# First rows of the input projection: modulation products of tiles 1 to 3 by column groups, x scaled on GpSimd ahead, and x issued before c

## The chip, the cores and the metric

The kernel runs on one core of a Trainium2 chip. The metric is the device time of one execution in microseconds (us); lower is better. TensorE (PE in the profile) does the matrix products, VectorE (DVE), ScalarE (ACT) and GpSimd (POOL) the elementwise work, and SyncE (SP) issues most transfers. "PEld" is the loading of a product's stationary operand, which runs beside the products.

## What is computed

One layer of a flow-matching backbone: adaLN modulation, one large input projection, a bidirectional state-space scan beside a gated MLP, and an output projection. Only the beginning matters here:

```python
sc = silu(c); scc = silu(c_ctx)
shift, scale, gate = split(sc @ w_ada + b_ada, 3)          # and the same from scc for the context
hc = rmsnorm(ctx, g_pre) * (1 + scale_c) + shift_c         # 256 context tokens
hx = rmsnorm(x, g_pre) * (1 + scale) + shift               # 256 latent tokens
zc = hc @ w_in[:, :XBC_W + DT_W];  zx = hx @ w_in          # D = 2048 is the contracted axis
```

Everything is float32. The 512 tokens (context in columns 0 to 255, latent in 256 to 511) are handled together, with the 2048 features cut into 16 tiles of 128 partitions.

## The kernel before

**Layout.** `xT` holds x transposed: 16 feature tiles of 128 x 512 tokens, loaded by four transfers of 1 MB. A product in full float32 precision is made from three faster ones: each operand is split into a rounded part "hi" and a remainder "lo", and hi*hi, hi*lo and lo*hi are added up in PSUM. So h (the normed and modulated x) exists as `hhi[k]` and `hlo[k]`, and a weight tile as `hi_st` and `lo_st`.

**Start.** ACT takes silu of c and c_ctx (`sc2`, 16 KB, into `sc`), which needs one table of functions, and then touches a square root so that the next table is in place. Then x is squared, even tiles on ACT and odd tiles on DVE (seven segments of the later buffer `y` in turn), and PE sums the squares over the features into `pss`, four tiles at a time in four column groups. Between these groups PE runs products that nobody reads (`warm`, tile `psw`). A small chain of transposes, a product `psb`, a root and a reciprocal leaves 1/rms of every token, spread over all partitions, in `rb` (a segment of `y`).

**Rows.** A "row" kt of the first stage is one feature tile: the products of its weights `wst[kt]` (960 columns: 64 for dt, then seven tiles of 128) with h of the same tile, added over all 16 rows in `psdt` (dt) and `psx[0..6]`. Step ("m", i) is one of these weight tiles, i = -1 being dt. Before a row can start, shift and scale of its 128 features must be known. They are products of `sc` with two chunks of `wada` (1 MB each) per tile. For tile 0 and, in pairs, for tiles 4 to 15 `ada_mm` makes them in four column groups of PE straight in PSUM (`psada`), and `ada_fin` reads them with a 32 x 32 block transpose on DVE (`adat`) and two small activations on ACT (`ha` = scale factor, `hb` = shift). For tiles 1 to 3 another way is taken: `ada_rows` multiplies four contracted tiles at once with 256 columns each, `ada_keep` copies the result to SBUF, `ada_sum` adds the four groups with two small products (tile `sel`), and `ada_one` makes `ha` and `hb`. Then `make_h(kt)` does, for the latent half and the context half: DVE xT = xT * ha * rb, ACT hhi = xT + hb, DVE hlo = (xT + hb) - hhi. `split_hi`, `split_dt` and `split_lo` cut the weights into hi and lo.

**Order.** On PE, DVE, ACT and POOL the instructions run in the order in which the program writes them (`manual_schedule`). `row_steps(kt)` gives the order inside row kt, in which the preparation of row n = kt + 1 is woven; NSING = 4 is the number of tiles whose shift and scale are made singly. SP issues its transfers in program order: c, x, then the chunks of `wada` and `wst` in the order of their use, with six buffers for `wada` and three for `wst`.

Of the kernel before, what the change touches and what calls it, by code (L numbers as in the profile page):

```python
# [8 lines left out]
F32 = mybir.dt.float32  # L9
# [3 lines left out]
ALU = mybir.AluOpType  # L13
# [31 lines left out]
def tile_hybrid_ssd_mlp(  # L45
# [126 lines left out]
    def spt(shape, name):  # L172
        return sps.tile(shape, F32, tag="s", name=name)
# [7 lines left out]
    sc2 = stp.tile([P, KT, 2], F32, name="sc2")  # L181
    nc.sync.dma_start(sc2, ccols)

# [25 lines left out]

    def ada_rows(c):  # L210

        u, k0 = c // 2, 8 * (c % 2)
        if k0 == 0:
            ada_ps[u] = spt([P, 512], f"psada{u}")
        ps = ada_ps[u]
        raw = ada_raw.pop(c)
        for kk in range(8):
            g = kk % 4
            nc.tensor.matmul(ps[32 * g : 32 * g + 32, 0:256], lhsT=sc[:, k0 + kk, :], rhs=raw[:, kk * 256 : (kk + 1) * 256],
                             start=k0 == 0 and kk < 4, stop=k0 > 0 and kk >= 4)  # L220

    def ada_keep(u):
        cp = st2.tile([P, 256], F32, tag="cp", name=f"adac{u}")
        nc.vector.tensor_copy(cp, ada_ps[u][:, 0:256])
        ada_ps[u] = cp, ada_ps[u][:, 256:260]

    def ada_sum(u):
        cp, pt = ada_ps[u]
        for q in range(2):
            nc.tensor.matmul(pt[:, 2 * q : 2 * q + 2], lhsT=cp[:, q * P : (q + 1) * P], rhs=sel[:, 0, 0:2],  # L230
                             start=True, stop=True)

    def ada_one(u):
        pt = ada_ps.pop(u)[1]
        nc.scalar.activation(ha[:, u, :], pt[:, 0:2], AF.Identity, bias=bsc1[:, u : u + 1],
                             scale=pc[:, C_GPRE + u : C_GPRE + u + 1])
        nc.scalar.activation(hb[:, u, :], pt[:, 2:4], AF.Identity, bias=pc[:, C_BADA + u : C_BADA + u + 1])

    def ada_mm(ci):
# [12 lines left out]
    def ada_fin(u):  # L252

        ps = ada_ps.pop(u)
        n = 64 * len(UNITS[u])
        ada_ps[u] = tr = st2.tile([P, 128], F32, tag="row", name=f"adat{u}")
        nc.vector.transpose(tr[:, 0:n], ps[:, 0:n])
        ada_ab(u, 0)

    def ada_ab(u, q):  # L260
        kt, tr = UNITS[u][q], ada_ps[u]
        nc.scalar.activation(ha[:, kt, :], tr[:, 64 * q : 64 * q + 2], AF.Identity, bias=bsc1[:, kt : kt + 1],
                             scale=pc[:, C_GPRE + kt : C_GPRE + kt + 1])
        nc.scalar.activation(hb[:, kt, :], tr[:, 64 * q + 32 : 64 * q + 34], AF.Identity,
                             bias=pc[:, C_BADA + kt : C_BADA + kt + 1])
# [7 lines left out]
    def wst_load(kt):  # L273
        w = st3.tile([P, WST], F32, tag="wst", name=f"wst{kt}")
        nc.sync.dma_start(w, wst[kt])
        wraw[kt] = w
# [11 lines left out]
    ada_load2(1)  # L288
    wraw[0] = st3.tile([P, WST], F32, tag="wst", name="wst0")
    for a, b in ((0, WH), (WH, WST)):  # L290
        nc.sync.dma_start(wraw[0][:, a:b], wst[0][:, a:b])
    ada_load(2)
# [10 lines left out]
    def warm(*ns):  # L303
        for n in ns:
            nc.tensor.matmul(psw[:, 0:n], lhsT=ones, rhs=ones[:, 0:1].to_broadcast([P, n]), start=True, stop=True)
# [26 lines left out]
    nc.vector.tensor_copy(ss4.rearrange("p (b i) -> p b i", i=32), bc(rc, 2, 32))  # L332
    nc.vector.transpose(rb, ss4)
    ada_mm(0)
    ada_mm(1)
    warm(512, 512)
    psdt = spt([P, TOK], "psdt")
# [20 lines left out]
    def split_lo(kt, a=64, b=WST):  # L358
        hi, lo = sp0[kt]
        nc.vector.tensor_tensor(lo[:, a - 64 : b - 64], wraw[kt][:, a:b], hi[:, 64 + a : 64 + b].bitcast(F32), op=ALU.subtract)  # L360

    def make_h(kt):
# [18 lines left out]
    def row_steps(kt):  # L381
# [31 lines left out]
    STEPS = {"a": ada_mm, "f": ada_fin, "f2": lambda u: ada_ab(u, 1), "r": ada_rows, "k": ada_keep, "g": ada_sum, "o": ada_one,  # L413
             "h": make_h, "c": split_hi, "d": split_dt, "l": split_lo,
             "l1": lambda n: split_lo(n, 64, WH), "l2": lambda n: split_lo(n, WH)}

# [29 lines left out]
    split_dt(0)  # L446
    make_h(0)
    split_lo(0, 64, WH)
# [813 lines left out]
def _layout(i):  # L1262
# [13 lines left out]
    for kt in range(NSING):  # L1276
        r = ss[:, :, :, kt] if kt == 0 else ss[:, :, :, kt].transpose(0, 1, 3, 2, 4)
        wada[2 * kt : 2 * kt + 2] = r.reshape(2, 8, P, 256).transpose(0, 2, 1, 3).reshape(2, P, D)
    for m in range(NSING, KT, 2):
# [49 lines left out]
```

## Time and profile before

| What | Value |
|---|---|
| median of 3 runs | 989.68 us (989.65 to 989.76) |
| profiled execution, first to last instruction (its span) | 987.9 us |
| the median run beyond that span | 1.8 us |
| PE busy in the span | 978.8 us, 99% |
| ACT, DVE, POOL busy | 495.4, 621.4, 112.5 us |
| transfers, 0 to 20 us and 20 to 60 us | 363 and 419 GB/s, the 16 DMA engines busy 0.91 of the time and all of it |

The profile's own time is its span; no other time is given for that execution, so the 1.8 us are the median run less the span, and stand for what lies before the first and after the last instruction. In the timelines the columns are: start in us, duration in us, engine, line, operation, output tile <- input tiles, shape, count of merged instructions, and in brackets how long the engine had been idle and what ended that.

### The profile page before, as it was taken

The page shows a single profiled execution, that of the slowest core. Times are in us where ns is not written, and L with a number is a line of the kernel's source. Part 1 is how long each engine was busy: PE and PEld are TensorE (multiplying, and loading weights), DVE is VectorE, ACT ScalarE, POOL GpSimd, SP SyncE. Part 2 cuts the span into 40 slices and gives each one's busy share as a digit, 9 for nine tenths or more (in the row PEclk, how much of TensorE's full clock was granted, in tenths as well). Part 3 has the DMA queues.
Part 4 walks back from the last instruction along what each step waited for, and adds up shares of the span by engine and source line. Part 5 has one row for each costly group of instructions (what it writes and reads, how often), then busy time and mean ns, then how long its engine had stood idle before and what let it go on. Part 6 is the DMA issues. An engine that isn't in the chain of part 4 may idle for free.

```text
span 987.9 us, 13929 instructions
## 1 busy us (share of the span) xinstructions
PE 978.8 (99%) x5502; PEld 792.6 (80%) x5502; DVE 621.4 (63%) x949; ACT 495.4 (50%) x762; POOL 112.5 (11%) x162
## 2 busy tenths in 40 slices
PE   9999999999999999999999999999999999999997
PEld 4688888778887878787888888887888888888885
DVE  4444488868886566756767766767555564445636
ACT  4233358566665554545445343454565563346522
POOL 0000002432453222224000000000000000000000
PEclk9999999999999999999999999999999999999999
DMA  9999844233323424145877768774455446556722
GB/s 372 421 418 418 352 149 166 86 129 128 128 75 139 142 98 145 43 169 206 297 302 284 275 257 296 280 274 170 170 180 203 171 170 213 178 206 228 282 86 85
DMA packets 31985, 207.26 MB, mean 210 GB/s; under 512 B 4128, under 2 KB 4384, under 8 KB 8496
## 3 DMA queue, kind: packets, MB, share of 16 engines
q1 hardware_dynamic: 29232, 192.79, 52.0%
q0 software_dynamic: 2112, 12.65, 3.7%
q8 instruction: 43, 0.70, 0.3%
q10 hardware_dynamic: 576, 0.94, 0.3%
q14 instruction: 22, 0.18, 0.1%
HBM read 204.20 MB, written 2.16 MB: 209 GB/s over the span
## 4 chain that ended last, share of the span: by engine, by line
PE 92%; DMA 4%; ACT 2%; DVE 1%; SPq 0%; issue 0%; ACTq 0%
PE pa L1108 12%; PE pa L1110 12%; PE pa L1109 12%; PE psx L141 9%; PE psx L143 9%; PE psx L142 9%; PE pm L1157 3%; PE pm L1155 3%; PE pm L1156 3%; DMA wst<-in_wst_dram 3%; PE pq L1157 2%; PE pq L1156 2%; PE pq L1155 2%; PE psada L249 2%; PE psc L778 1%; PE pso L831 1%
## 5 line engine op out<-in xcount | busy, mean ns | idle before, releaser
L85 DVE TENSOR_TENSOR lo_w<-w,hi_w 128x1024 fp32r<-128x1024 f32 x173 | 210.7, 1224 | 146.0 <-ACT hi_w L84 145.9
L84 ACT CAST hi_w<-w 128x1024 fp32r<-128x1024 f32 x173 | 182.1, 1053 | 204.5 <-PE pa L1110 129.4
L1108 PE MATMUL pa<-hi_w,hhi 128*128 128x512 f32 x512 | 202.3, 395 | 0.0
L1110 PE MATMUL pa<-hi_w,hlo 128*128 128x512 f32 x512 | 199.5, 390 | 0.0
L1109 PE MATMUL pa<-lo_w,hhi 128*128 128x512 f32 x512 | 199.3, 389 | 0.0
L141 PE MATMUL psx<-hhi,hi_w 128*128 128x512 f32 (+1 forms) x400 | 153.4, 383 | 0.0
L143 PE MATMUL psx<-hhi,lo_w 128*128 128x512 f32 (+1 forms) x400 | 145.9, 365 | 0.0
L142 PE MATMUL psx<-hlo,hi_w 128*128 128x512 f32 (+1 forms) x400 | 145.7, 364 | 0.0
L1108 PEld LDWEIGHTS pa<-hi_w,hhi 128*128 128x128 f32 x512 | 96.2, 188 | 20.5 <-issue 1.6
L1110 PEld LDWEIGHTS pa<-hi_w,hlo 128*128 128x128 f32 x512 | 96.1, 188 | 20.3
L1109 PEld LDWEIGHTS pa<-lo_w,hhi 128*128 128x128 f32 x512 | 96.2, 188 | 19.5 <-issue 0.2
L576 DVE SCALAR_TENSOR_TENSOR xbc<-psx,pc,xbc 128x248 f32<-128x248 f32 (+1 forms) x204 | 83.6, 473 | 34.8 <-ACT xbc L560 33.9
L501 DVE TENSOR_TENSOR lo_w<-w,hi_w 128x1024 fp32r<-128x1024 f32 x61 | 77.1, 1271 | 23.7 <-ACT hi_w L495 23.6
L141 PEld LDWEIGHTS psx<-hhi,hi_w 128*128 128x128 f32 x400 | 75.5, 189 | 13.4 <-issue 2.9
L143 PEld LDWEIGHTS psx<-hhi,lo_w 128*128 128x128 f32 x400 | 75.4, 188 | 12.5
L142 PEld LDWEIGHTS psx<-hlo,hi_w 128*128 128x128 f32 x400 | 75.6, 189 | 12.2 <-issue 1.7
L495 ACT CAST hi_w<-w 128x1024 fp32r<-128x1024 f32 x61 | 63.5, 1044 | 26.0 <-PE psx L142 12.9
L966 DVE SCALAR_TENSOR_TENSOR junk<-gate,cb 128x2048 bf16<-128x2048 f32 x16 | 36.7, 2291 | 24.1 <-DMA gate<-in_wada_dram 24.1
L1155 PE MATMUL pm<-hi_w,hhi 128*128 128x512 f32 x128 | 50.0, 390 | 0.0
L1156 PE MATMUL pm<-lo_w,hhi 128*128 128x512 f32 x128 | 49.9, 390 | 0.0
L1157 PE MATMUL pm<-hi_w,hlo 128*128 128x512 f32 x128 | 49.7, 389 | 0.0
L730 ACT ACTIVATE R<-R,y 128x128 f32<-128x128 f32 x128 | 38.8, 391 | 0.0
(248 smaller groups left out, 1333.6 us busy)
## 6 DMA issues: line engine op xcount, KB each, us to landing
w<-in_wlat_dram SPq DMA_DIRECT2D x64, 1024.0 KB, 4.8
w<-in_wout_dram SPq DMA_DIRECT2D x32, 1024.0 KB, 4.8
ada<-in_wada_dram SPq DMA_DIRECT2D x30, 1024.0 KB, 13.4
w<-in_wxbc_dram SPq DMA_DIRECT2D x25, 1024.0 KB, 4.8
gate<-in_wada_dram SPq DMA_DIRECT2D x16, 1024.0 KB, 5.5
R<-acs POOLq DMA_DIRECT2D x8, 1024.0 KB, 5.2
wst<-in_wst_dram SPq DMA_DIRECT2D x15, 480.0 KB, 14.0
xT<-in_xch_dram SPq DMA_DIRECT2D x4, 1024.0 KB, 8.0
```

Of the source, the lines that this page charges most:

```text
L84: nc.scalar.copy(hi, raw)
L85: nc.vector.tensor_tensor(lo, raw, hi.bitcast(F32), op=ALU.subtract)
L141: nc.tensor.matmul(ps, lhsT=whi, rhs=hhi[k][:, s], start=start, stop=False)
L142: nc.tensor.matmul(ps, lhsT=whi, rhs=hlo[k][:, s], start=False, stop=False)
L143: nc.tensor.matmul(ps, lhsT=wlo, rhs=hhi[k][:, s], start=False, stop=stop)
L576: nc.vector.scalar_tensor_tensor(ao, zi, cw[:, k : k + 1], ao, op0=ALU.mult, op1=ALU.add)
L1108: nc.tensor.matmul(pa[tk], lhsT=hhi[k][:, t], rhs=whi[:, w], start=k == 0, stop=False)
L1109: nc.tensor.matmul(pa[tk], lhsT=hhi[k][:, t], rhs=wlo[:, w], start=False, stop=False)
L1110: nc.tensor.matmul(pa[tk], lhsT=hlo[k][:, t], rhs=whi[:, w], start=False, stop=k == KT - 1)
L1155: nc.tensor.matmul(p, lhsT=yh[:, t], rhs=whi[:, w], start=j == 0, stop=False)
L1156: nc.tensor.matmul(p, lhsT=yh[:, t], rhs=wlo[:, w], start=False, stop=False)
L1157: nc.tensor.matmul(p, lhsT=yl[:, t], rhs=whi[:, w], start=False, stop=hf == 0 and j == 15)
```

## The change

Five things are changed, all of them ahead of row 4.

1. Tiles 1 to 3 take the way of tile 0: `ada_mm` with 64 columns and four column groups, `ada_fin` with the transpose from PSUM. `ada_rows`, `ada_keep`, `ada_sum` and `ada_one` go. For tiles 0 to 3 `ha` is now made on DVE, while ACT makes `hb`.
2. xT * rb of tiles 0 to 3 is done on GpSimd (`scale_x`), queued right behind the making of `rb`.
3. For tiles 0 to 3 `make_hs` replaces `make_h`: ACT hhi = xT * ha + hb in one activation; DVE makes the same value in float32 (`full`, a segment of `y`) and subtracts.
4. The order in rows 0 to 3 is another: row 0 has products by token halves and a list of its own (`row0`), and in rows 1 and 2 both chunks of the next tile, `ada_fin`, h and the splits stand behind weight tile 4 (`m[:6]`); the weight transfers of tiles 1 to 3 are issued in two parts.
5. c (`sc2`) is issued from ACT, behind `pc`; x is now SP's first transfer. The last `warm` before row 0 has 256 columns in place of 512.

```diff
-    nc.sync.dma_start(sc2, ccols)
+    nc.scalar.dma_start(sc2, ccols)
...
-    def ada_rows(c):
...
-    def ada_keep(u):
...
-    def ada_sum(u):
...
-    def ada_one(u):
...
     def ada_fin(u):
...
         nc.vector.transpose(tr[:, 0:n], ps[:, 0:n])
-        ada_ab(u, 0)
+        if u < NSING:
+            nc.vector.tensor_scalar(ha[:, u, :], tr[:, 0:2], pc[:, C_GPRE + u : C_GPRE + u + 1], bsc1[:, u : u + 1],
+                                    op0=ALU.mult, op1=ALU.add)
+            nc.scalar.activation(hb[:, u, :], tr[:, 32:34], AF.Identity, bias=pc[:, C_BADA + u : C_BADA + u + 1])
+        else:
+            ada_ab(u, 0)
...
     def wst_load(kt):
         w = st3.tile([P, WST], F32, tag="wst", name=f"wst{kt}")
-        nc.sync.dma_start(w, wst[kt])
+        for a, b in ((0, WH), (WH, WST)) if kt < NSING else ((0, WST),):
+            nc.sync.dma_start(w[:, a:b], wst[kt][:, a:b])
...
+    def scale_x(kt):
+        for s in TH:
+            nc.gpsimd.tensor_tensor(xT[:, kt, s], xT[:, kt, s], rb[:, s], op=ALU.mult)
+
+    TH = (slice(256, 512), slice(0, 256))
+    for kt in range(2):
+        scale_x(kt)
     ada_mm(0)
     ada_mm(1)
-    warm(512, 512)
+    warm(512, 256)
...
+    def make_hs(kt):
+        full = yseg(2 + kt % 2)
+        for v, s in enumerate(TH):
+            nc.scalar.activation(hhi[kt][:, s], xT[:, kt, s], AF.Identity, bias=hb[:, kt, v : v + 1],
+                                 scale=ha[:, kt, v : v + 1])
+        for v, s in enumerate(TH):
+            nc.vector.tensor_scalar(full[:, s], xT[:, kt, s], ha[:, kt, v : v + 1], hb[:, kt, v : v + 1],
+                                    op0=ALU.mult, op1=ALU.add)
+            nc.vector.tensor_tensor(hlo[kt][:, s], full[:, s], hhi[kt][:, s].bitcast(F32), op=ALU.subtract)
...
+        if n == 1:
+            return [("o", 0), m[5], ("a", 2), m[4], ("a", 3), ("c1", 1), ("f", 1), ("d", 1), ("hs", 1), ("l1", 1),
+                    ("c2", 1), ("l2", 1), m[6], m[7]]
         if n < NSING:
-            r = [("r", 2 * n), ("r", 2 * n + 1)]
-            g = m[4:5] + [("g", n), ("o", n), h_]
-            if n < 3:
-                q = 5 - n
-                return m[:q] + r + [c_, ("k", n), d_, ("l1", n)] + g + [("l2", n)] + m[q:4] + m[5:]
-            return m[:3] + r + s_ + [("k", n)] + g + m[3:4] + m[5:]
+            return m[:6] + [("a", 2 * n), ("a", 2 * n + 1), ("x", n), ("c1", n), ("f", n), ("d", n), ("hs", n),
+                            ("l1", n), ("c2", n), ("l2", n)] + m[6:]
...
+    def row0(kt):
+        whi, wlo = sp0[kt]
+        for v, s in enumerate(TH):
+            nc.tensor.matmul(psdt[:, s], lhsT=whi[:, 0:P], rhs=hhi[kt][:, s], start=v == 0, stop=False)
+            for i in range(3):
+                nc.tensor.matmul(psx[i][:, s], lhsT=whi[:, (i + 1) * P : (i + 2) * P], rhs=hhi[kt][:, s],
+                                 start=v == 0, stop=False)
+        dt_mm(kt, 1)
+        for i in range(3):
+            nc.tensor.matmul(psx[i], lhsT=whi[:, (i + 1) * P : (i + 2) * P], rhs=hlo[kt], start=False, stop=False)
+        for i in range(3):
+            nc.tensor.matmul(psx[i], lhsT=wlo[:, i * P : (i + 1) * P], rhs=hhi[kt], start=False, stop=False)
```

How the order on the engines changes, at three places. First the head of ACT's program, up to the squares of x, in the changed kernel (its line numbers are its own; `sc2` is printed as sc_161):

```order
L104 DMA pc_87<-in_pcols_dram 128x304
L182 DMA sc2_161<-in_ccols_dram 128x32
L272 ACT_TABLE_LOAD
L272 ACTIVATE sc_159<-sc2_161 128x16x2
L273 ACT_TABLE_LOAD
L273 ACTIVATE sc2_161<-epsc_157 128x1
L290 ACTIVATE y_68<-xT_156 128x512 x8
```

The second row is new on this engine; before, it was SP's first transfer, ahead of the four of xT.

Then DVE in the changed kernel, from the transpose that makes rb (first row) to the last split of row 0's weights (wst0, hi_st0 and lo_st0 are the weights of row 0; y is here `full`, or rb in the first row):

```order
L308 STREAM_TRANSPOSE y_68<-y_68 128x512
L228 STREAM_TRANSPOSE adat0_328<-psada0_251 128x64
L230 TENSOR_SCALAR ha_111<-adat0_328,pc_87,bsc1_112 128x2
L338 TENSOR_TENSOR hi_st0_325<-wst0_177,hi_st0_325 128x64
L350 TENSOR_SCALAR y_68<-xT_156,ha_111,hb_110 128x256
L352 TENSOR_TENSOR hlo0_133<-y_68,hhi0_117 128x256
L350 TENSOR_SCALAR y_68<-xT_156,ha_111,hb_110 128x256
L352 TENSOR_TENSOR hlo0_133<-y_68,hhi0_117 128x256
L342 TENSOR_TENSOR lo_st0_326<-wst0_177,hi_st0_325 128x384
L342 TENSOR_TENSOR lo_st0_326<-wst0_177,hi_st0_325 128x512
```

Before, two products of three operands and two subtractions stood in the place of the four rows of L350 and L352, and `ha` was ACT's. POOL's eight products of `scale_x` follow one another beside these rows.

Last PE in the changed kernel, from the end of row 1 to the start of row 2 (psada2 belongs to tile 2, hhi1 to row 1, hhi2 to row 2):

```order
L143 MATMUL psx4_323<-hhi1_118,lo_st1_436 128x512
L220 MATMUL psada2_482<-ada_4_188,sc_159 32x64 x32
L220 MATMUL psada2_482<-ada_5_190,sc_159 32x64 x32
L141 MATMUL psx5_324<-hhi1_118,hi_st1_435 128x512
L142 MATMUL psx5_324<-hlo1_134,hi_st1_435 128x512
L143 MATMUL psx5_324<-hhi1_118,lo_st1_436 128x512
L141 MATMUL psx3_322<-hhi1_118,hi_st1_435 128x256
L142 MATMUL psx3_322<-hlo1_134,hi_st1_435 128x256
L143 MATMUL psx3_322<-hhi1_118,lo_st1_436 128x256
L422 MATMUL psdt_318<-hhi2_119,hi_st2_549 128x512
L439 MATMUL psx0_319<-hhi2_119,hi_st2_549 128x512
L440 MATMUL psx0_319<-hhi2_119,lo_st2_550 128x512
```

Before, the products of tile 2 stood behind weight tile 1 and a pair of 128 x 2 products (`ada_sum`) followed three products behind them, with half of row 1 still to come; now six products of row 1 lie between the last product of tile 2 and the first that needs its h.

More of the change, by code (lines that the diff above doesn't have):

```diff
@@ L208, in tile_hybrid_ssd_mlp @@
     ada_ps = {}
-    def ada_rows(c):
[L212 to L220, printed above, removed]
-    def ada_keep(u):
-        cp = st2.tile([P, 256], F32, tag="cp", name=f"adac{u}")
-        nc.vector.tensor_copy(cp, ada_ps[u][:, 0:256])
-        ada_ps[u] = cp, ada_ps[u][:, 256:260]
-    def ada_sum(u):
[L228 to L231, printed above, removed]
-    def ada_one(u):
[L234 to L237, printed above, removed]
     def ada_mm(ci):
@@ L288, in tile_hybrid_ssd_mlp @@
     ada_load2(1)
-    wraw[0] = st3.tile([P, WST], F32, tag="wst", name="wst0")
-    for a, b in ((0, WH), (WH, WST)):
-        nc.sync.dma_start(wraw[0][:, a:b], wst[0][:, a:b])
+    wst_load(0)
     ada_load(2)
@@ L446, in tile_hybrid_ssd_mlp @@
     split_dt(0)
-    make_h(0)
+    make_hs(0)
     split_lo(0, 64, WH)
@@ L1276, in _layout @@
     for kt in range(NSING):
-        r = ss[:, :, :, kt] if kt == 0 else ss[:, :, :, kt].transpose(0, 1, 3, 2, 4)
-        wada[2 * kt : 2 * kt + 2] = r.reshape(2, 8, P, 256).transpose(0, 2, 1, 3).reshape(2, P, D)
+        wada[2 * kt : 2 * kt + 2] = ss[:, :, :, kt].reshape(2, 8, P, 256).transpose(0, 2, 1, 3).reshape(2, P, D)
     for m in range(NSING, KT, 2):
```

4 lines of the change are left out of this document (2 added, 2 removed).

## The prediction

> **What bounds the kernel now.** I read the chain of waits on the page first, then the engines' busy time in the stretch behind the changed rows, then the timeline from 0 to 60 us. The page and the stretch (its columns: time on PE, PEld, DVE, ACT, POOL, each with its count, then granted clock, DMA share, GB/s):
>
> ```profile
> span 987.9 us, 13929 instructions
> PE 92%; DMA 4%; ACT 2%; DVE 1%; SPq 0%; issue 0%; ACTq 0%
> 60.00:130.00 70.00, 69.95 (x894) 60.00 (x893) 33.96 (x70) 28.31 (x56) 0.00 (x0) 1.00 0.91 375
> ```
>
> PE has 92% of the chain, and behind the changed rows it works 69.95 of 70.00 us at full clock. Nothing there can give time back: what PE loses or wins by row 3 reaches the end whole. The sum is made against the profiled execution (span 987.9); the median, 989.68, lies 1.8 us above it, and I add the same 1.8.
>
> A win has a ceiling, though. Row 5's weights come off a stream of transfers that has no pause yet:
>
> ```profile
> 57.38 0.99 ACT L352 CAST hi_st<-wst 128x960 fp32r<-128x960 f32 x1 [0.60 <-DMA wst<-in_wst_dram]
> 59.69 0.19 PEld L436 LDWEIGHTS psx<-hhi,lo_st 128*128 128x128 f32 x1 [0.33 <-DVE lo_st L360]
> ```
>
> ACT waited 0.60 us for those weights, and PE's loads 0.33 us for what DVE made of them. Rows that start earlier only meet this wait earlier. The stream itself moves up by no more than the place that c leaves at SP's head (x now starts at 1.25, c at 0.81, in rows below): 0.44 us. So no version of these rows can win more than about 0.4.
>
> **The change part by part. First, c behind pc.** The beginning:
>
> ```profile
> 0.81 0.38 SPq L182 DMA_DIRECT2D sc<-in_ccols_dram  x1
> 0.81 0.41 ACTq L104 DMA_DIRECT2D pc<-in_pcols_dram  x1
> 1.25 2.09 SPq L279 DMA_DIRECT2D xT<-in_xch_dram  x4
> 3.02 1.28 ACT L297 ACT_TABLE_LOAD   x1 [3.02 <-DMA sc<-in_ccols_dram]
> 5.86 0.20 ACT L298 ACTIVATE sc<-epsc 128x1 f32<-128x1 f32 x1
> 6.17 1.15 ACT L315 ACTIVATE y<-xT 128x512 f32<-128x512 f32 x2
> 6.95 1.61 PE L317 MATMUL pss<-y,ones 128*32 128x512 f32 x8
> 8.75 1.15 ACT L315 ACTIVATE y<-xT 128x512 f32<-128x512 f32 x2 [1.44 <-DMA xT<-in_xch_dram]
> 15.13 1.07 PE L317 MATMUL pss<-y,ones 128*32 128x512 f32 x8
> 18.67 0.71 DVE L333 STREAM_TRANSPOSE y<-y 128x512 f32<-128x512 f32 x1
> ```
>
> ACT loads its first table only when c has landed (3.02), and the two tables, silu and the touch of the root end at 5.86 + 0.20 = 6.06. So from c's landing to the first square of x lie 3.04 us, and x lands just then (first square 6.17): in this kernel the two are balanced. In the changed one c is ACT's second transfer, issued at about 0.81 + 0.41 + 0.05 = 1.27, when SP has issued the first MB of x (0.81) and is issuing the second: four issues in 2.09 us are 0.52 each with their gaps, so about 1.3. When does c land?
>
> It is 16 KB, with three bounds. Low: with nothing before it, as now, 2.2 us after issue, at 3.45. Middle: behind one MB of x, which lands 0.44 earlier than now, at about 5.7. High: behind two, 8.75 - 0.44 = 8.3. Two places in the middle of the kernel show what a small or young transfer does when another queue is full. The first has `gate` on SP's queue while q0 (loads of POOL) is at work, the second `G` on POOL's queue while q1 is:
>
> ```profile
> 463.90 0.33 SPq L78 DMA_DIRECT2D gate<-in_wada_dram  x1
> q0 software_dynamic: 242, 0.80, 93.7%
> gate<-in_wada_dram SPq DMA_DIRECT2D x1, 1024.0 KB, 6.7
> 643.88 0.54 POOL L974 DMA_DIRECT2D G<-in_gpost_dram  x1 [80.51 <-ACT hi_w L84]
> q1 hardware_dynamic: 106, 0.87, 78.8%
> G<-in_gpost_dram POOLq DMA_DIRECT2D x1, 1024.0 KB, 7.4
> ```
>
> In the three microseconds from 463.9 only q0 moved a packet, in those from 643.9 only q1; the younger transfer landed 6.7 and 7.4 us after its issue. So the older work is finished first, and c doesn't slip between x's packets: I rule the low bound unlikely. Between middle and high the two issues are about 0.03 us apart, a tie by the rows. c is spread over the 16 engines and has landed when the last share has; one engine that takes x's second tile first is enough for 8.3. I take the high bound.
>
> [...] The trace at 463.9 speaks against strict turns: q1 had work and got none for 3 us.
>
> By the high bound ACT is free at 8.3 + 3.04 = 11.35 in place of 6.06, the first square shifts from 6.17 to 11.35, and PE's first sum of squares from 6.95 to about 12.1. Nothing is caught up: PE's three groups from 6.95 to 15.13 take 2.7 us each with the unread products between them, ACT's two squares of a group 1.15, and x is long there. The last group and with it `rb` (19.38 = 18.67 + 0.71) shift by **5.2 us**. By the middle bound ACT is free at 8.8, the shift is 2.6; by the low one 6.5, and 0.3.
>
> **Second, row 0.** Now from `rb` (call it R, 19.38) to the product of row 1 that waits for nothing more, 31.38, are 12.0 us. The rows of the operations that replace or join those of today:
>
> ```profile
> 19.75 0.25 DVE L257 STREAM_TRANSPOSE adat<-psada 128x64 f32<-128x64 f32 x1 [0.37 <-PE psada L249]
> 20.33 0.28 ACT L264 ACTIVATE hb<-adat,pc 128x2 f32<-128x2 f32 x1
> 20.46 0.88 DVE L365 SCALAR_TENSOR_TENSOR xT<-xT,ha,y 128x256 f32<-128x256 f32 x2
> 21.04 0.91 ACT L368 ACTIVATE hhi<-xT,hb 128x256 fp32r<-128x256 f32 x2 [0.43 <-DVE xT L365]
> 21.58 0.89 DVE L370 SCALAR_TENSOR_TENSOR hlo<-xT,hb,hhi 128x256 fp32r<-128x256 f32 x2 [0.24 <-ACT hhi L368]
> 31.38 0.39 PE L436 MATMUL psx<-hhi,lo_st 128*128 128x512 f32 x1
> 31.61 0.40 PE L418 MATMUL psdt<-hlo,hi_st 128*128 128x512 f32 x1
> L614 DVE TENSOR_SCALAR y<-y 128x256 f32<-128x256 f32 x1 | 0.3, 286 | 0.0
> L823 POOL TENSOR_TENSOR y<-xk,dsk 128x256 f32<-128x256 f32 x16 | 9.5, 610 | 0.0
> 181.72 2.48 POOL L707 TENSOR_TENSOR xw<-xk,ed 128x256 f32<-128x256 f32 x4
> 182.14 2.21 DVE L814 SCALAR_TENSOR_TENSOR M<-cbf,dtt,M 128x128 f32<-128x128 f32 x4
> L814 DVE SCALAR_TENSOR_TENSOR M<-cbf,dtt,M x64: 339/346/698, 182.1 to 452.4; 128x128 f32<-128x128 f32 x64
> ```
>
> DVE's two products (0.88) leave; POOL makes them at 0.61 each, so the two tiles that follow R take 4 x 0.61 = 2.4 us; those of tiles 2 and 3 come in their rows and have time. DVE's new `full` is priced by L614, 0.29 each: 0.57 more than nothing, where the products saved 0.88. By these rows alone row 0 would shorten: ACT needs only POOL's half and `hb`, and I get R + 10.35, a win of 1.65 (hhi starts 0.6 earlier than behind two products of DVE, and lo_st 1.05 earlier than behind two hlo of 0.89).
>
> [...] The four L814 that lie beside POOL's products at 182.14 take 2.21 us, 0.55 each, where their median is 346 ns; one took 698. [...] Turn by turn, with one POOL product between two of DVE: transpose and ha end at R + 0.85, the split of dt 0.6 later; hhi ends at R + 1.4 and R + 2.0; two full (0.29) and two hlo (0.48, each with a wait of 0.61) end DVE's h at R + 4.15; lo_st of 0.55 and 0.68 with what is left of POOL's at R + 5.05 and R + 6.1; PE's products of the three weight tiles that need lo_st at R + 9.1, and the product of row 1 that stands at 31.38 now at R + 11.85, 12.0 now: **-0.15**. The bounds are -1.65 (no lock) and +1.7 (all of POOL's go first); I take the turns, since the four at 182.14 show neither a standstill nor free running.
>
> **Third, rows 1 to 3.**
>
> ```profile
> 28.80 0.55 DVE L360 TENSOR_TENSOR lo_st<-wst,hi_st 128x384 fp32r<-128x384 f32 x1
> 38.31 0.40 PE L418 MATMUL psdt<-hhi,hi_st 128*128 128x512 f32 x1
> 42.72 0.61 PE L230 MATMUL psada<-sel,adac 128*128 128x2 f32 x4
> 45.71 0.40 PE L418 MATMUL psdt<-hhi,hi_st 128*128 128x512 f32 x1
> ```
>
> A row takes 45.71 - 38.31 = 7.40 us now without a wait. The small sums (0.61 on PE) go, with a copy on DVE; that the products of the next tile are now 64 columns wide I take as no difference (at worst it eats the 0.6). But they moved to the end of the row. What follows their last product is a chain: transpose (0.25), hb (0.28), two hhi (0.91), a full and two hlo (0.29 + 0.48), lo_st (0.55), 2.76 us together. PE has six products of row 1 to run meanwhile, three of 512 columns at the pitch of 31.61 - 31.38 = 0.23 and three of 256 at half of it (1.05), then two of row 2 (0.46) and about 0.25 for handing over, before it needs lo_st: 1.75. PE stands for 1.0 and has saved 0.6: **+0.45 for a row**, twice **+0.9** (the third such row, row 1, is in the second part). Today the 3.0 us from L230 (42.72) to the next row (45.71) hide the shorter chain behind it; that cover is gone. The bounds: -0.6 (lo_st, whose weights lie there, made before h after all) and +1.0 (nothing saved). The smaller `warm` and the split transfers of wst are free: both lie beside the chain to `rb`.
>
> Sum: 987.9 + 5.2 - 0.15 + 0.9 + 1.8 = **995.6 us**.
>
> **Rivals.** *c behind one tile of x only:* 2.6 in place of 5.2: 993.1. For it speaks that the two issues nearly tie; against it that all 16 shares must win the tie. *The clock falls:* with the high bound PE stands idle from 7.0 to 12.1. Before its first warm-up its products are slower:
>
> ```profile
> 4.70 0.34 PEld L305 LDWEIGHTS psw<-ones 128*128 128x128 f32 x1 [0.52 <-issue]
> 5.55 0.21 PEld L305 LDWEIGHTS psw<-ones 128*128 128x128 f32 x1 [0.52 <-issue]
> 6.00 0.19 PEld L305 LDWEIGHTS psw<-ones 128*128 128x128 f32 x1 [0.24 <-issue]
> ```
>
> The pitch is 0.85 us up to 5.55 and 0.45 from there. The slow stretch is at most 5.55 - 0.81 = 4.7 us long; run again, it loses 1 - 0.45/0.85 = 0.47 of that, 2.2 us: 997.9. Nothing in the rows shows so long a pause of PE, so I can't say whether it cools. [...]
>
> *The other side, no loss:* c lands early (3.45), from its place on a queue of its own with little in it; then the first part gives +0.3, the second, without the lock, -1.65, the third +0.9, and the ceiling leaves -0.4 of their sum: 989.3; with the turns of row 0 kept it is +1.05, 990.7. It decides where c lands before about 3.5. Against it stand 463.9 and 643.9. *The change does not do what it says:* POOL's products so hinder DVE that x ahead costs as much as it saves; that is the +1.7 above, 997.4 with the high bound.
>
> **How the numbers follow.** High bound 0.40, one tile 0.25, with a cold clock 0.15, c early 0.17, anything else (POOL first) 0.03. The time is that of the likeliest, 995.6. The range reaches from the middle of the early case, 990.0, to the cold one with some slack, 998.2. About 0.2% (2.0 us) is what a measurement of this kernel can tell from no change: the slower cases are 0.40 + 0.25 + 0.15 less 0.08 for a smaller shift, with the other 0.03: 0.75. Early c is mostly within 2.0: with those 0.08 it makes 0.21 for the same, and 0.04 is left for faster, since the ceiling allows it only if the stream should move up more than I see.
>
> **What would show it.** In the changed profile the row of ACT's first table load names c and its time: 8.3 (one tile: 5.7; early: 3.4). PE's first sum of squares stands at 12.1, the transpose that makes `rb` ends at 24.6. The granted clock between 12 and 17 tells the cold case. POOL's eight products behind `rb` and the length of DVE's beside them (over 0.5 us, where alone 0.3) show the lock. From the first psdt of row 2 to that of row 3 should be 7.85 us with PE waiting for `lo_st` or `hhi` for about 1.0. Wrong would be: a first square before 8.5, no wait of PE at the heads of rows 2 and 3, or a wait at row 5 longer than now.

## The result, and the profile after

The changed kernel takes 1001.67 us (median of 4 runs, 1000.76 to 1002.44) where the kernel before takes 989.72: a ratio of 1.0116, with a 95% interval of 1.0104 to 1.0129. It is slower, as forecast in sign, but by about twice the amount (11.5 us by the ratio, 11.95 by the medians, 5.9 forecast) and outside the range. The ratios here and below leave out one execution at a reduced clock, of the kernel before with 64-column products (1222.79 us at a granted clock of 0.75, one of six). The profiled execution of the changed kernel took 1000.76, with this span and chain of waits on the page:

```profile
span 999.0 us, 14523 instructions
PE 93%; DVE 2%; ACT 2%; DMA 1%; issue 1%; ACTq 0%; SPq 0%; DVEq 0%
```

PE still carries the chain, but DVE and "issue" have a larger part in it (1% and 0% before) and DMA a smaller one (4% before): "issue" is time in which the engine waited for nothing that the profile shows. The timeline of the changed kernel, at the places where the loss arises (line numbers are its own):

```profile
1.25 0.45 ACTq L182 DMA_DIRECT2D sc<-in_ccols_dram  x1
9.02 1.28 ACT L272 ACT_TABLE_LOAD   x1 [9.02 <-DMA sc<-in_ccols_dram]
12.63 2.44 PE L292 MATMUL pss<-y,ones 128*32 128x512 f32 x8 [5.18 <-ACT y L290]
25.82 0.71 DVE L308 STREAM_TRANSPOSE y<-y 128x512 f32<-128x512 f32 x1
26.68 6.83 POOL L311 TENSOR_TENSOR xT<-xT,y 128x256 f32<-128x256 f32 x8 [23.67 <-DVE y L308]
27.56 0.72 DVE L350 TENSOR_SCALAR y<-xT,ha,hb 128x256 f32<-128x256 f32 x1
30.01 0.76 DVE L352 TENSOR_TENSOR hlo<-y,hhi 128x256 fp32r<-128x256 f32 x1
30.69 2.23 DVE L342 TENSOR_TENSOR lo_st<-wst,hi_st 128x384 fp32r<-128x384 f32 x2
30.82 0.50 PE L422 MATMUL psdt<-hlo,hi_st 128*128 128x512 f32 x1 [1.26 <-DVE hlo L352]
39.28 0.50 PE L440 MATMUL psx<-hhi,lo_st 128*128 128x512 f32 x1 [0.56 <-DVE lo_st L342]
45.26 0.41 PE L220 MATMUL psada<-ada,sc 128*32 128x64 f32 x11 [0.80 <-issue]
47.54 0.50 PE L422 MATMUL psdt<-hhi,hi_st 128*128 128x512 f32 x1 [0.63 <-ACT hhi L347]
48.95 0.50 PE L440 MATMUL psx<-hhi,lo_st 128*128 128x512 f32 x1 [0.67 <-DVE lo_st L342]
57.45 0.50 PE L440 MATMUL psx<-hhi,lo_st 128*128 128x512 f32 x1 [0.56 <-DVE lo_st L342]
```

The first product of each row that needs `lo_st` (L440, before the change L436) makes a good milestone. Before, it stands at 31.38, 38.78, 46.18 and 55.01 for rows 1 to 4; now at 39.28, 48.95, 57.45 and 66.37. The rows of these that neither stand above nor in the prediction (L436 before, L440 after):

```profile
38.78 0.39 PE L436 MATMUL psx<-hhi,lo_st 128*128 128x512 f32 x1
46.18 0.39 PE L436 MATMUL psx<-hhi,lo_st 128*128 128x512 f32 x1
55.01 0.40 PE L436 MATMUL psx<-hhi,lo_st 128*128 128x512 f32 x1
66.37 0.40 PE L440 MATMUL psx<-hhi,lo_st 128*128 128x512 f32 x1
```

| Stretch | before | after | lost |
|---|---|---|---|
| start to `rb` | 19.38 | 26.53 | 7.15 |
| `rb` to row 1's milestone | 12.00 | 12.75 | 0.75 |
| row 1 to row 2 | 7.40 | 9.67 | 2.27 |
| row 2 to row 3 | 7.40 | 8.50 | 1.10 |
| row 3 to row 4 | 8.83 | 8.92 | 0.09 |

These sum to 11.36; the span grew by 11.1, since the wait for weights at row 5 (0.33) is gone. Nothing is lost or won later.

The first stretch falls into two. PE's first sum of squares moved from 6.95 to 12.63, by 5.68, because c landed at 8.94 and ACT's first table load began at 9.02. From there to `rb` it was 12.43 and is now 13.90, 1.47 more. The granted clock is in the third column from the right. The first row is the kernel before, the other two the changed kernel:

```profile
12.00:18.00 6.00, 6.00 (x67) 2.42 (x69) 2.77 (x6) 1.88 (x4) 0.00 (x0) 1.00 0.99 394
6.00:12.00 6.00, 1.45 (x3) 0.21 (x1) 2.79 (x7) 2.94 (x5) 0.00 (x0) 0.82 1.01 424
12.00:18.00 6.00, 5.37 (x20) 1.56 (x20) 1.29 (x2) 3.28 (x7) 0.00 (x0) 0.61 1.00 397
```

In the changed kernel PE worked 1.45 of the 6 us from 6 to 12, and the granted clock was 0.61 in the next six, where it was 1.00 before.

### The profile page after: what moved, and what is told of

Read it like the earlier page. It is cut to its first block, busy times and chain, and to the rows that moved or that the text cites. A ratio compares the mean times of both kernels' runs of the same rounds, so it can differ in the third digit from the quotient of the medians.

```text
span 999.0 us, 14523 instructions
## 1 busy us (share of the span) xinstructions
PE 980.0 (98%) x5782; PEld 794.6 (80%) x5782; DVE 623.8 (62%) x954; ACT 494.5 (50%) x761; POOL 119.3 (12%) x170
## 4 chain that ended last, share of the span: by engine, by line
PE 93%; DVE 2%; ACT 2%; DMA 1%; issue 1%; ACTq 0%; SPq 0%; DVEq 0%
PE pa L1112 12%; PE pa L1113 12%; PE pa L1114 12%; PE psx L141 9%; PE psx L143 9%; PE psx L142 9%; PE pm L1159 3%; PE pm L1161 3%; PE pm L1160 3%; PE psada L220 3%; PE pq L1161 2%; PE pq L1159 2%; PE pq L1160 2%; PE psc L782 1%; PE pso L835 1%; PE psy L861 1%
## 5 line engine op out<-in xcount | busy, mean ns | idle before, releaser
L580 DVE SCALAR_TENSOR_TENSOR xbc<-psx,pc,xbc 128x248 f32<-128x248 f32 (+1 forms) x204 | 83.6, 472 | 34.8 <-ACT xbc L564 33.9
```

What stands on the lines that cost most here:

```text
L580: nc.vector.scalar_tensor_tensor(ao, zi, cw[:, k : k + 1], ao, op0=ALU.mult, op1=ALU.add)
```

## The experiments

Three theories were tested first: late c (with a cold clock behind it), the rows' own waits, and the transfers' queue. Each ratio is to executions of the kernel before that were made along with that experiment, whose medians lie between 989.78 and 990.49; compare experiments by their ratios.

**c first again, all else as changed.**

```diff
-    nc.scalar.dma_start(sc2, ccols)
+    nc.sync.dma_start(sc2, ccols)
```

> The changed kernel with one edit undone: c is SP's first transfer again, ahead of x. Theory L (late c): c lands near 3.0 in place of 8.94, rb ends near 19.4 in place of 26.5, and 7.2 us of the 12.0 go; the rest of the loss, about 4.1 us by the row starts, stays: about 994. Rival R (rows): the late start is mostly slack that rows 1 to 3 would have lost to their own waits anyway (h and lo_st at the head of each row, transfers that wait for buffers), and the time stays above 998. Rival Q (queue): the waits of rows 1 and 2 are themselves an effect of the late start, because SP stood 5.9 us for row 0's lo_st; then they go too and the time falls to 991 or less.

Measured: 994.89, ratio 1.0043 (1.0026 to 1.0059). The edit of c thus costs some 7 us of the 11.5 (1.0116 less 1.0043), as the table says. The rest stays, so rivals R and Q both fall. In this profile c is back, but PE pauses longer inside the products of tile 2, and then its clock falls, to a mean of 0.55 from 42 to 48 us:

```profile
3.04 1.28 ACT L272 ACT_TABLE_LOAD   x1 [3.04 <-DMA sc<-in_ccols_dram]
38.77 0.41 PE L220 MATMUL psada<-ada,sc 128*32 128x64 f32 x11 [1.52 <-issue]
42.00:48.00 6.00, 5.80 (x16) 4.32 (x15) 1.02 (x2) 0.00 (x0) 0.00 (x0) 0.55 1.01 412
```

The profiled execution was the longest of the four (996.53; the shortest 993.94), and such a fall of the clock fits a scatter of that size. The mean clock of the four executions goes with it: 0.996, 0.997, 0.998 and 0.999 for 996.53, 995.64, 994.14 and 993.94 us. That it is the cause was not tested.

**Only c behind pc, on the kernel before.**

```diff
-    nc.sync.dma_start(sc2, ccols)
+    nc.scalar.dma_start(sc2, ccols)
```

> The kernel before with one edit of the change alone: c is issued by ACT behind pc. Theory L: c lands near 8.9, first square of x near 12, rb shifts by 7.2 as in the changed kernel, and the time is 989.7 + 7.2 = 996.9. Rival (c lands in time when nothing else is changed, or the rows take up the shift): below 992.

Measured: 995.91, ratio 1.0057 (1.0042 to 1.0072): one moved line of 16 KB costs 5.6 us by itself (6.9 in the profiled execution, the longest of the four, by its span of 994.8). c lands as late as in the changed kernel, PE's clock halves, and rows 1 to 3 keep their 7.50 and 7.40 us:

```profile
9.30 1.28 ACT L297 ACT_TABLE_LOAD   x1 [9.30 <-DMA sc<-in_ccols_dram]
12.00:18.00 6.00, 5.08 (x12) 1.56 (x12) 1.29 (x2) 3.56 (x8) 0.00 (x0) 0.50 1.01 420
```

With the 4.3 of the experiment before (the change without this line) it makes 9.9 of 11.5. Each of the three has an interval of more than 1 us to either side, so the remaining 1.6 us are not clear of the noise.

**c ahead of pc on ACT.** Changed kernel, the two issues of ACT exchanged:

```diff
+    nc.scalar.dma_start(sc2, ccols)
     nc.scalar.dma_start(pc, pcols)
...
-    nc.scalar.dma_start(sc2, ccols)
```

> The changed kernel with ACT's two transfers exchanged: c first, pc second; x stays SP's first. Theory of turns (an engine finishes a tile of x, then takes one transfer of the other queue, then the next tile): c lands where pc lands now, at 6.4, and pc at about 8.9; ACT is free at 9.5, rb shifts by 4 to 4.5 rather than 7.15, PE idles about 2.7 us and stays warm: about 998. Theory of arrival: c comes at the same moment as x's first tile and shares with it, lands before 4, and the time is that of c first or lower, 993 to 994.

Measured: 998.61, ratio 1.0081 (1.0066 to 1.0096). c landed with the first tile of x, not before it, as the theory of turns has it (how long a turn is, the last experiment tells). That PE would stay warm was wrong: it idled only 2.07 us, and the clock was halved right behind, from 10.5 to 13.9 us:

```profile
6.22 1.28 ACT L272 ACT_TABLE_LOAD   x1 [6.22 <-DMA sc<-in_ccols_dram]
10.50:13.90 3.40, 3.40 (x8) 1.00 (x5) 2.47 (x6) 2.10 (x4) 0.00 (x0) 0.50 1.01 426
```

**PE kept at work until c is there.**

```diff
     warm(512, 512, 512, 512)
+    warm(*[512] * 6)
```

> The changed kernel with six more unread products (512 columns, about 0.87 us each warm) behind the first four, so that PE works through its pause from 6.86 to 12.63. Theory C (cold clock): the granted clock from 12 to 18 is 1.00 in place of 0.61, the first group of sums and its unread products take 2.6 to 3.0 us in place of 4.67, and the time falls by 1.3 to 2.2, to about 999.5 to 1000.4, with less scatter between runs. Rival: the clock is not what makes that stretch long, and the time stays within 0.5 of 1001.7 or grows.

Measured: 1000.88, ratio 1.0107 (1.0092 to 1.0123), just above the range expected, and not clear of the changed kernel's 1.0116 (1.0104 to 1.0129). The clock theory holds for its stretch: the clock stays at 1.00, and `rb` ends at 25.30 in place of 26.53. But something took most of the 1.2 us back: PE's pause that waits for nothing grew from 0.80 to 3.02 us and moved, from the products for tile 2's shift and scale to a product of row 0's weight tile 5.

```profile
12.00:18.00 6.00, 4.93 (x22) 1.61 (x23) 2.14 (x4) 4.42 (x10) 0.00 (x0) 1.00 1.00 419
38.31 0.39 PE L142 MATMUL psx<-hlo,hi_st 128*128 128x512 f32 x1 [3.02 <-issue]
```

That a pause moves when products are added far ahead of it suggests that it hangs on a count. So the next theory, K, was that PE stops for its own code.

**Rows 1 and 2 prepared early.** c first, and:

```diff
-            return m[:6] + [("a", 2 * n), ("a", 2 * n + 1), ("x", n), ...] + m[6:]
+            return m[:2] + [("a", 2 * n), ("a", 2 * n + 1), ("x", n), ...] + m[2:]
```

> c first on SP as in the first experiment, and in rows 1 and 2 the whole preparation of the next tile stands behind two steps of the row (dt and weight tile 0) in place of six. Theory H (heads of rows): PE's waits at the heads of rows 2 and 3 (1.5 us each for hhi and lo_st) go, so 2 x 1.5 us less, and the clock, which fell to 0.55 from 42 to 48 us there, stays at 1.00 (up to 2.3 more): 990.5 to 992. Rival K (code): PE's pause inside the products of tile 2 is where the time goes; the heads matter little, the pause stays at the same count of instructions or longer, and the time is above 993.

Measured: 994.42, ratio 1.0043 (1.0029 to 1.0057): nothing won. The waits at the heads of rows 2 and 3 are gone, as theory H wants, but the pause of PE grew to 3.31 us, as rival K wants.

**GpSimd held back in row 0.** c first, and GpSimd's products of tile 1 (and all behind them) wait for row 0's splits:

```diff
-    for kt in range(2):
-        scale_x(kt)
+    scale_x(0)
...
     split_lo(0, WH)
+    nc.gpsimd.tensor_copy(scr, sp0[0][1][:, WST - 65 : WST - 64].bitcast(F32))
+    scale_x(1)
```

> c first on SP, and GpSimd's four products of tile 1 wait (behind a one-element copy of the last column of row 0's lo_st) until DVE has finished row 0's splits. Theory P (DVE and GpSimd exclude each other): DVE's full, hlo and lo_st of row 0 fall from 0.72-0.82, 0.77 and 1.15 us to about 0.41, 0.43 and 0.6, PE's wait for the second hlo (1.4) shrinks by 0.8 or more, and row 1 starts 0.8 to 1.3 earlier: 993.5 against 994.9. Rival: only GpSimd is slowed, DVE keeps its lengths, no change within 0.5.

Measured: 992.17, ratio 1.0024 (1.0015 to 1.0033); without the edit it was 1.0043 (1.0026 to 1.0059), so the gain in time is at the edge of the noise. Row 1 starts 1.25 us earlier (29.52 for 30.77), within what was expected. The timeline of row 0:

```profile
20.29 0.72 DVE L349 TENSOR_SCALAR y<-xT,ha,hb 128x256 f32<-128x256 f32 x1
21.12 0.42 DVE L351 TENSOR_TENSOR hlo<-y,hhi 128x256 fp32r<-128x256 f32 x1
21.46 0.41 DVE L349 TENSOR_SCALAR y<-xT,ha,hb 128x256 f32<-128x256 f32 x1
22.32 1.15 DVE L341 TENSOR_TENSOR lo_st<-wst,hi_st 128x384 fp32r<-128x384 f32 x2
23.67 4.19 POOL L311 TENSOR_TENSOR xT<-xT,y 128x256 f32<-128x256 f32 x6
```

With GpSimd at rest, DVE's `full`, `hlo` and the two `lo_st` take 0.41, 0.42 and 1.15 us (the first `full`, 0.72, still lies beside the two products of tile 0, which end at 20.86); beside it they took 0.72 to 0.82, 0.76 and 2.23. GpSimd's products are hindered too: six take 4.19 here, 0.70 each, where the eight of the changed kernel took 6.83, 0.85 each. Theory P holds as far as these lengths go: each engine's operations are longer beside the other's. That the two exclude each other was not shown. The heads of rows keep their waits. This profile has no pause for code, which would account for more than P alone was to win.

**The kernel before with 64-column products for tiles 1 to 3**, at their old places (`ada_mm` and `ada_fin` in place of `ada_rows`, `ada_keep`, `ada_sum` and `ada_one`, with the order of `wada` in memory that goes with them):

```diff
-            r = [("r", 2 * n), ("r", 2 * n + 1)]
-            g = m[4:5] + [("g", n), ("o", n), h_]
+            r = [("a", 2 * n), ("a", 2 * n + 1)]
+            g = m[4:5] + [("f", n), h_]
```

> The kernel before with one part of the change alone: tiles 1 to 3 by column groups (64 products of 64 columns and the transpose from PSUM), at the places in rows 0 to 2 where their products stood before. Theory K (code): PE runs 128 instructions more per tile, its code is fetched in pieces of 16 KB behind 1 MB transfers, and a pause of PE of 0.8 to 2 us that waits for nothing in the records appears in rows 1 or 2, ending 1.3 us behind a piece; net of the 0.6 us per row of the small sums the time is 989.5 to 991.5. Rival: no pause, and 3 x 0.6 us are saved up to the ceiling of the transfers: 989.2 to 989.5.

Measured: 993.02, ratio 1.0031 (1.0019 to 1.0044), slower than K had priced it: there are two pauses "issue" (0.87 us at 38.51 and 1.42 at 46.15), and at the head of row 1 PE waits 1.85 us for `hhi`. That wait comes from DVE's order: the transpose of tile 1 stands behind a split of the weights, whose rounding on ACT waited for their transfer until 27.64, while tile 1's products were done at about 27.4.

```profile
29.28 0.24 DVE L257 STREAM_TRANSPOSE adat<-psada 128x64 f32<-128x64 f32 x1
31.52 0.50 PE L418 MATMUL psdt<-hhi,hi_st 128*128 128x512 f32 x1 [1.85 <-ACT hhi L368]
```

The saving of 0.6 us a row on the small sums is lost in these waits.

Now the count. A window from the start to just before the pause gives PE's products and loads so far (the numbers behind x). In order: the changed kernel, the one with six more unread products, the one with early rows and GpSimd held back (below), and the one just told:

```profile
0.00:45.20 45.20, 35.56 (x477) 19.35 (x478) 18.18 (x37) 12.94 (x24) 9.20 (x23) 0.92 0.94 376
```

```profile
0.00:38.20 38.20, 31.55 (x350) 15.71 (x351) 17.78 (x37) 12.83 (x24) 9.21 (x23) 1.00 0.96 387
```

```profile
0.00:37.50 37.50, 31.77 (x477) 17.34 (x478) 19.09 (x46) 15.36 (x28) 8.16 (x24) 1.00 0.96 386
```

```profile
0.00:46.00 46.00, 39.78 (x605) 23.77 (x606) 19.94 (x45) 16.21 (x30) 2.37 (x15) 0.96 0.97 393
```

477 + 478 = 955, 701, 955, 1211: the pauses stand at steps of 254 to 256 instructions, whatever PE is doing there and whenever it gets there. (The other pauses fit: 955 with c first and with c ahead of pc, 956 for the earlier one of the kernel just told.) Counted with PE's few semaphore instructions, which these columns leave out, they stand at 705, 961 and 1217, exactly 256 apart. And each is preceded by one packet on a queue of its own; in the changed kernel, in the window from 42.6 to 43.9:

```profile
q8 instruction: 1, 0.02, 5.3%
```

A packet of that queue is 16 KB (45 of them make 0.74 MB in the changed kernel's page, as the next fence shows), and PE goes on at 45.26, some 1.4 us behind its end; over all eight pauses, in seven kernels, that distance is 1.3 to 1.5.

```profile
q8 instruction: 45, 0.74, 0.3%
```

The profile calls this queue `instruction`. The kernel before has 43 of its packets for PE's 5502 products and as many loads, the changed kernel 45 for 5782 and as many: 256 and 257 instructions a packet. So I read a packet as a block of PE's code, 256 instructions long, which is an inference from these counts and from the pauses 256 apart. In the eight pauses crossing into the next block costs 0.8 to 3.3 us. The 64-column products burn 256 instructions in about 2 us (128 products and as many loads; in row 2 they run without a pause from 52.26 to 54.18), while in those pauses PE went on only 3.8 to 7.6 us behind the step before.

**Early rows and GpSimd held back together** (the two diffs above).

> The edits of the two experiments on rows 1 and 2 and on GpSimd together, c first on SP. Theories H and P together: row 1 starts 1 us earlier than in the first experiment and no heads wait; with the pause for code of 1 to 2 us left, 990 to 991.5, and no better than 989.3 since the transfers cap it. If it stays above 993 neither of the two is what the rows lose.

Measured: 993.86, ratio 1.0039 (1.0024 to 1.0054), worse than expected: no head of rows 2 and 3 waits, but the pause is 3.27 us, and the clock is halved behind it:

```profile
37.67 0.39 PE L142 MATMUL psx<-hlo,hi_st 128*128 128x512 f32 x1 [3.27 <-issue]
38.00:41.40 3.40, 3.40 (x11) 2.75 (x10) 0.00 (x0) 0.57 (x1) 0.00 (x0) 0.50 1.02 425
```

**Row 0's part alone on the kernel before:** `scale_x(0)`, `make_hs(0)`, `row0` and the shorter unread product; tiles 1 to 3 in the old way:

```diff
-    warm(512, 512)
+    scale_x(0)
+    warm(512, 256)
...
-    make_h(0)
+    make_hs(0)
...
-                return m[:q] + r + [c_, ("k", n), ...
+                return ([("row0", 0)] if n == 1 else m[:q]) + r + [c_, ("k", n), ...
```

> The kernel before with the row 0 part of the change alone: x/rms of tile 0 on GpSimd (two products, none behind them), hhi by one activation, products by token halves; c first on SP and rows 1 to 3 in the old way. Theory P (the loss of row 0 came from GpSimd's products of tile 1 beside DVE): row 1 starts at about 29.4 in place of 30.81, rows 1 to 3 keep their 7.40, row 5 waits for its weights longer by what was won, and the time is 989.3 to 989.6, no better than 0.4 below the kernel before. Rival: row 0 itself is slower in the new form, row 1 starts no earlier and the time is 990 or more.

Measured: 990.09 against 990.04 of its own runs of before, ratio 1.0000 (0.9991 to 1.0009). The time is the rival's, but not for its reason: row 0's own products end earlier, but PE then meets the transfer of tile 1's weights of `wada`, and row 1 starts at 30.71 (30.81 before):

```profile
26.45 0.64 PE L219 MATMUL psada<-ada,sc 128*32 128x256 f32 x8 [0.62 <-DMA ada<-in_wada_dram]
```

**The same instructions, 124 places on.** The kernel with early rows and GpSimd held back, and at the start:

```diff
-    warm(512, 512, 512, 512)
+    warm(512, 512, 512)
+    for j in range(32):
+        g = j % 4
+        nc.tensor.matmul(psw[32 * g : 32 * g + 32, 0:64], lhsT=ones[:, 0:32], ...)
```

> The kernel with rows 1 and 2 early and GpSimd's products of tile 1 late (993.86), with one of the four unread products at the start replaced by 32 small unread ones, which moves every later instruction of PE 124 places on and changes nothing behind them. Theory K (code comes in pieces of 256 instructions, and PE pauses where it reaches the end of a piece less than about 6 us after the end of the last): the limits 705 and 961 fall 124 instructions earlier in the work, the second into the middle of tile 2's products with the first far ahead of it; the pause of 3.5 us there goes or shrinks below 1, and the time is 990 to 991.3. Rival (the pause belongs to the products of tile 2, a wait that the records hide): it stays where it is in the work, 3 us or more, and the time is 993 to 994.

Measured: 990.08, ratio 1.0000 (0.9991 to 1.0009), from 1.0039. 32 unread products at the start, which do nothing, win 3.8 us: the pause is gone, and with it the halved clock behind it (1.00 from 38.0 to 41.4). This is the test of theory K, since nothing else differs behind them. It is also the whole change but for the edit of c and the places of two edits, and it is as fast as the kernel before, not faster. Where rows 3 and 4 start, and the waits from there to row 5:

```profile
44.91 0.40 PE L425 MATMUL psdt<-hhi,hi_st 128*128 128x512 f32 x1
49.97 0.81 PEld L220 LDWEIGHTS psada<-ada,sc 128*32 128x32 f32 x32 [0.22 <-DMA ada<-in_wada_dram]
54.34 0.50 PE L425 MATMUL psdt<-hhi,hi_st 128*128 128x512 f32 x1 [0.28 <-ACT hhi L363]
57.28 0.99 ACT L337 CAST hi_st<-wst 128x960 fp32r<-128x960 f32 x1 [0.47 <-DMA wst<-in_wst_dram]
59.59 0.19 PEld L443 LDWEIGHTS psx<-hhi,lo_st 128*128 128x128 f32 x1 [0.34 <-DVE lo_st L345]
```

Row 3 starts 0.80 ahead of the kernel before (45.71), row 4 only 0.20 (54.54), row 5 0.11 (59.06 for 59.17). PE meets the transfer of `wada` in row 3 (49.97), and ACT that of row 5's weights (57.28, where it was 57.38): the transfers take the win back before it can be kept.

**x's first MB in rows of 2 KB**, on the changed kernel:

```diff
+    for k in range(4):
+        nc.sync.dma_start(xT[:, k, :], xch[0][:, k * TOK : (k + 1) * TOK])
-    for t in range(4):
+    for t in range(1, 4):
```

> The changed kernel with the first MB of x in four transfers, so that its rows are 2 KB long in place of 8; bytes, order and everything else as they are. Theory T (the engines change between the two queues packet by packet, so each of the 16 small rows that pc and c put on an engine waits for one row of x, 0.31 us for 8 KB): pc lands near 4.5 and c near 5 to 6 (16 turns of about 0.08 to 0.13 us, some of them beside rows of x's second tile), ACT is free 3 to 4 us earlier, and the time falls by 3 to 5, to 997 to 998.5. Theory A (the older transfer is finished first, c comes behind two tiles of x whatever their rows): c lands at 8.7 to 9 as now and the time stays within 1 of 1001.7.

Measured: 996.39, ratio 1.0067 (1.0050 to 1.0083), 5 us better than the changed kernel. c landed 3.2 us earlier although it was issued where it was and the bytes ahead of it are the same:

```profile
5.83 1.28 ACT L274 ACT_TABLE_LOAD   x1 [5.83 <-DMA sc<-in_ccols_dram]
```

The landing alone would not settle it: shorter pieces also mean more issues, so that x's second tile is issued at 2.66 in place of 1.24, now behind c. The packets do. In the changed kernel, from 3 to 6 us, the two queues moved nearly the same number of packets (SP's and ACT's; packets, MB, share):

```profile
q1 hardware_dynamic: 152, 1.11, 88.8%
q10 hardware_dynamic: 150, 0.15, 14.1%
```

From 6 to 8 us, when c's rows move, it is 106 and 106. In the 0.355 us from 3.402, in pc's stretch, each queue moved 16, and in the 0.32 us from 6.80, in c's, again 16 and 16; a row of 8 KB takes 0.31 us by its record, one of pc 0.05 and one of c 0.01. If age decided, the younger queue would stand still there; instead the two take turns row by row. Spread evenly, each of the 16 engines has 8 rows of pc and 8 of c (128 rows each), and every one waits for a row of x: 8 KB, 64 KB per engine and tile. So pc lasts as long as the first tile of x and c as long as the second, though c is 128 bytes a row. A turn here is one row, even a row of 128 bytes.

## Why the prediction was wrong in size

**The bound, right.** PE carries the chain and what is lost by row 4 reaches the end whole (11.36 there, 11.1 in the span). The ceiling on a win held too: the padded kernel, whose row 3 starts 0.80 earlier, ends at a ratio of 1.0000. Row 0 alone met a transfer earlier still, that of tile 1's `wada`.

**c behind pc, right in place, by a wrong reason.** I chose the high bound, 8.3, and c landed at 8.94. The step "the older work is finished first" failed: turns of rows put c behind two tiles of x, so that the place was right by luck. x's first tile, issued 0.44 earlier, landed no earlier (6.2, where it was 6.1), with pc's rows between its own; the bounds had counted on that 0.44. The two windows at 463.9 and 643.9 did not show what I read in them; why only one queue moved there stays open. The term was 5.2, and PE's first sum shifted by 5.68.

**The clock, a rival that should have been a term.** I gave it a chance of 0.15 as an alternative to the high bound, although the high bound brings the idle stretch of more than 5 us with it. The stretch lost 1.47 (2.2 forecast for that case), and the run that filled the pause got 1.2 of it back.

**Row 0, mis-sized.** -0.15 was forecast and 0.75 lost. That GpSimd's products lengthen DVE's operations is shown (`hlo` 0.42 us without them, 0.76 beside them). That each `hlo` waits out a whole product of GpSimd, the 0.61 in the sum of turns, no run shows: it took 0.34 longer, and `full` 0.31 to 0.41. Two other numbers were wrong as well: GpSimd runs all eight products in one go (6.83 us) and not four with the rest later "in their rows", since nothing makes it wait; and `full` takes 0.41 alone and not 0.29. It reads one tile only, besides two columns of factors, and was slowed as well (0.72 to 0.82), so that the slowing is not confined to operations that read two tiles.

**Rows 1 to 3, the chain right and too short.** Forecast were 0.45 a row from a wait of 1.0 us. The rows show two waits, for `hhi` (0.63 to 0.66) and for `lo_st` (0.56 to 0.67), and the product behind each wait takes 0.50 us in place of 0.39 to 0.40, with the next 0.33 to 0.34 behind its start in place of 0.23: row 2 to row 3 lost 1.10, net of the 0.6 saved. I had let PE start its row on time (with 0.25 for handing over, an estimate that no row gives) and wait only once, and the chain behind the products is longer: 3.13 us in row 2, from the transpose (54.32) to the product that needs `lo_st` (57.45), where 2.76 were forecast from the last product. Moved early, the waits are gone.

**What was missing: PE's code.** The sum had no term for it, and I called the narrower products "no difference". The changed kernel has 280 more products, and in the profiled execution the pause cost about 1.09 of the 2.27 us of row 1: tile 2's products took 3.01 us (42.59 to 45.60), tile 3's 1.92 (52.26 to 54.18). With all of it the sum is 995.65 + 0.48 (c) + 1.47 (clock) + 0.90 (row 0) + 1.47 (heads of rows) + 1.09 (code) - 0.33 (no wait at row 5) = 1000.73, against 1000.76 of that execution. This is bookkeeping, since the terms are read off the same execution; the experiments show that each is there. Only the price of the heads of rows stands in the timeline alone, since moving them early won no time while the pause grew. So the failed step is the sum itself: it held the clock apart as a rival though it comes with the late c (1.47), sized row 0 at -0.15 for 0.75 and a row's head at 0.45 for about 1.1, and had no term for code (1.09).

The length of the pause, 0.8 to 3.3 us at the same count, follows in these traces, in the main, from how fast PE gets from one step of 256 to the next. The packet for the next block sets out only behind the last step (1.4 to 5.1 us in the eight pauses), and PE can go on 3.8 to 7.6 us behind that step, 5.0 to 6.1 in six of the eight. Where PE needed 2.4 us for its 256 instructions (both kernels with early rows and no padding) the pause was 3.3; where it needed 4.15 (the changed kernel, c first, c ahead of pc) it was 0.8 to 1.7. In the padded kernel the steps lie 5.9 us and more apart, and nothing is left to wait for. With GpSimd held back PE needed some 4 us, and the block came just in time (a packet between 33.7 and 34.8). What makes the packet set out early or late stays open.

## What to carry to other kernels

In these traces a small transfer on a second queue pays one row of the big stream for each of its own rows (16 packets against 16 in 0.355 us, 0.31 us for a row of 8 KB): send first what an engine's first instruction needs, or keep the stream's rows short while it is under way (with rows of 2 KB c landed 3.2 us earlier here). Count PE's instructions as well as its columns: here PE paused 0.8 to 3.3 us in or behind a burst of many narrow products, when 256 instructions were run in 2.4 to 4.2 us beside full transfer engines (0.94 to 0.97 busy from the start to the pause), and the sign of it is an idle time that waits for nothing at counts 256 apart. An engine that nothing holds back runs ahead, and the engine that works beside it can pay for what it does there: here GpSimd ran eight products in one go (6.83 us), and DVE's operations beside them took 1.8 to 2 times as long.

## What the hardware showed unexpectedly

- PE paused 0.80 to 3.3 us at 701, 955 and 1211 instructions, 1.3 to 1.5 us behind a 16 KB packet of the queue `instruction`; the packet set out only behind the step of 256 before. 124 instructions put in front took a pause of 3.27 us away and 3.8 us off the time.
- Two queues shared the transfer engines row by row (152 and 150 packets in 3 us), 8 KB against 1.2 KB: 16 KB in rows of 128 bytes landed 7.7 and 8.0 us after their issue behind pc, 4.5 us with 2 KB rows of x beside them, and 2.1 us when they were first.
- After more than 5 us without work PE's granted clock was 0.50 to 0.61 in the window from 12 to 18 us; shorter pauses were followed by a fall too (3.84 of 6 us at work from 36 to 42, with c first: 0.55; one pause of 2.07, with c ahead of pc: 0.50), but a pause of 2.88 with 2 KB rows was not (1.00 from 4.7 to 20). The length of a pause alone does not decide it.
- DVE's operations on SBUF took 1.8 to 2 times as long beside GpSimd's (0.42 to 0.76, 0.41 to 0.82, 1.15 to 2.23 us), and GpSimd's 1.2 times (0.70 to 0.85 us).
